# Two-block mixer: the first block's scores on stacked float32r operands, A heads between their projections, output weights read by halves

## The chip, the cores and the metric

The kernel runs on one core of a Trainium2 chip. The metric is device time in microseconds for one execution. PE is TensorE's matmul stream, PEld its weight loads, DVE VectorE, ACT ScalarE, POOL GpSimd and SP the engine that issues most loads. TensorE is granted one of two clock levels, 1.2 or 2.4 GHz; the profile shows the granted share, 0.50 or 1.00.

## The reference

512 tokens of width 1024 pass a first block and then a larger second block. Only the first block changes here. Its mixer has 8 "A" heads and 8 "B" heads of 64 features (B: two groups with one key/value head each). Cut to what matters:

```python
aq, ak, av, bq, kc, vc, ksl, vsl, kw, vw, gl = split_columns(rms_norm(h) @ w_in)
o_a  = mixer_dilated(aq, ak, av)               # three dilations, 8 heads
o_c  = softmax(bq @ compress(kc).T) @ compress(vc)     # 31 compressed tokens
o_s  = softmax(bq @ ksl.T + bias) @ vsl                # selected blocks
o_w  = softmax(bq @ kw.T + bias) @ vw                  # window of 512
o_b  = sum of the three, weighted by gates of gl
h    = h + concat(o_a, o_b) @ w_out
h    = h + (silu(n @ w_gate) * (n @ w_up)) @ w_down     # n = rms_norm(h)
```

With 512 tokens every A head and every B branch is a causal softmax over 512 keys with a bias by distance, so all three kinds run through the same routine.

## The kernel before, in words

The products of the projections keep float32 accuracy by splitting each operand in a high and a low float32r part and adding three products (`mm3`, L154 to L156). The attention scores before the change don't: they are plain float32 products, which the trace shows as two PE instructions each.

The first block (`first_block`) goes in this order. The rows are normed and turned. `proj_N` makes the A values. `bias_rows` writes the bias of every head, skewed for later reads, to DRAM: four stores on ACT's own queue. Eight `proj_T` make the A queries `aqT` and keys `akT` (128 features, that is two heads, by 512 tokens); queries leave PSUM by one ACT instruction (L283), keys by one copy on whichever engine is chosen (L286). The accumulators have two PSUM buffers, the split weights four.

`heads_a(p)` attends query tiles 2p and 2p+1 of the A heads, two heads (e = 0, 1) at a time. For a query tile i, `scores` (L373) makes the products with (i+1) x 128 keys (L377: 64 rows of the array, since a head has 64 features), adds the bias and takes the minimum on DVE (L382), the exponential on ACT (L383), turns the result on PE (L198) and copies it (L388). `values` multiplies with the values (L402), turns the reciprocal sums (L198) and splits the result for `w_out` on ACT and POOL (`split_late`). A pair is the four scores of two heads and two query tiles: widths 128, 128, 256, 256 at p = 0 and 384, 384, 512, 512 at p = 1. `attend` runs the turns a few scores late and slips the products with the values between the next scores.

After `heads_a(0)` come the windows of the compressed branch, the four B query projections `bqT`, `compress`, the gates, `heads_c` (scores against 32 compressed keys), and the keys `kslT` and `kwT`. Then one stream: `heads_a(1)`, `heads_b(0)` (8 pairs, two branches for each t), `heads_b(1)`. In `heads_b(0)`, `second_region` frees the A operands, loads the residual rows X (one 2 MB load on SP's queue) and makes `oc`, the compressed branch's output, in one go (`compressed`, L454, 32 rows of the array). `w_out(0)` and the feed-forward operand of the first 256 tokens stand at n = 3 of `heads_b(1)`, `w_out(1)` after it. Each `w_out(p)` reads all eight 512 KB chunks of the output weights, 16 chunk reads and splits in all, and adds both halves of the mix in one accumulation.

The written order is one of priority. The framework places the instructions of every engine ahead of time and lets later work fill an engine's gaps; products of `w_out(0)`, written in `heads_b(1)`, run between scores of `heads_a(1)`. Pools are buffers under a tag: an instruction that needs a buffer waits until an earlier user has released it. The feed-forward (from 433 us) also makes the modulation vectors of the second block, long vector work on DVE and POOL.

The second block's layers already use the stacked form: `stack_q`, `stack_k` and `qk` (L864) exist and serve their attention.

Of the kernel before, what the change touches and what calls it, by code (L numbers as in the profile page):

```python
# [77 lines left out]
class Act:  # L78
    """an operand with features on partitions, split in two exact parts; 512 lat tokens and 256 ctx tokens"""
# [15 lines left out]
class Kit:  # L95
    """Pieces shared by all phases: weight streaming, exact splits, products, norms."""
# [104 lines left out]
# =====================================================================  first block  # L201
def normed_T(K, ps_t, xs, nt, g, dst):
    """xs: normed rows of nt token tiles; transposed, times g per feature, split"""
# [11 lines left out]
def first_block(K, st, h_es):  # L215
    """x -> the first block's output in DRAM (K.dx), and the operand of layer 0's projections"""
# [34 lines left out]
    att = K.pool(att_es, "b1a")  # L251
    ap = K.pool(a_es, "b1ap", side="right")
# [20 lines left out]
    aqT = ap.tile([P, 4, S], F32, name="aqT")  # L273
    akT = ap.tile([P, 4, S], F32, name="akT")
    av = ap.tile([P, NT, 512], F32, name="av")
    bqT = proj.tile([P, 4, S], F32, name="bqT")
    kslT = proj.tile([P, S], F32, name="kslT")
    kwT = proj.tile([P, S], F32, name="kwT")
# [3 lines left out]
    def qevac(dst):  # L282
        return lambda ps: nc.scalar.activation(dst, ps, AF.Copy, scale=-0.125)  # L283

    def cevac(dst):
        return lambda ps: nc.any.tensor_copy(dst, ps)  # L286

    # ---- bias of every head by distance, for the skewed reads below
# [18 lines left out]
    # ---- compressed tokens: windows of 32 keys through a small MLP  # L307
# [6 lines left out]
    kcT = proj.tile([P, 32], F32, name="kcT")  # L314
# [5 lines left out]
    def windows(b):  # L320
        """overlapping windows of the raw keys or values, with their positions added"""
        cmpx = att.tile([P, 2, 512], F32, name="cmpx", tag="mhi", bufs=3)
# [9 lines left out]
        cmp[b] = att.tile([P, D], F32, name="blk", tag="mlo", bufs=3)[:, :992].rearrange("p (j g n) -> p j g n", j=16, g=2)  # L332
# [5 lines left out]
    def compress(b):  # L338
# [14 lines left out]
        if b == 0:  # L353
            for g in range(2):
                nc.tensor.matmul(ps2[64 * g:64 * g + 64, :32], cw2[:, 0], hid[:, g, 0], start=True, stop=True)
            nc.vector.tensor_copy(kcT, ps2[:, :32])
# [8 lines left out]
    def bias_tile(h, p):  # L365
        """(128, 256*(p+1)): negated bias of q tile 2p+1 against keys up to it"""
# [6 lines left out]
    def scores(qrow, krow, wb, i, fill, pt, den):  # L373
        """exponentials of q tile i of one head, transposed; fill puts work between"""
        w, ii = P * (i + 1), i % 2
        ps = ps_s.tile([P, 512], F32, name="sps", tag="s")
        nc.tensor.matmul(ps[:, :w], qrow[:, i * P:(i + 1) * P], krow[:, :w], start=True, stop=True)  # L377
# [12 lines left out]
    def pair(qT, ks, wbs, p, fill):  # L390
        """scores of two heads, q tiles 2p and 2p+1"""
        pts = [att.tile([P, 2 * p + 2, 256], F32, name="pt", tag="pt", bufs=4, padded_shape=[P, 4, 256]) for _ in range(2)]
        den = small.tile([P, 2, 2], F32, name="den", tag="den4", bufs=4)
        return [scores(qT[64 * e:64 * e + 64], ks[e], wbs[e], 2 * p + i, fill, pts[e], den[:, i, e:e + 1])
# [12 lines left out]
    def mix_tile(half, p):  # L407
        mix[half, p] = [att.tile([P, 4, 256], F32R, name=n, tag=n, bufs=3) for n in ("mhi", "mlo")]
        return mix[half, p]

    def heads_a(p, fill):
        m = mix_tile(0, p)

        def values(t, pts, den):
# [3 lines left out]
            split_late(K, m[0][:, t], m[1][:, t], weigh(K, att, po, rw))  # L418

        for t in range(4):  # L420
            sc, pts, den = pair(aqT[:, t], [akT[64 * e:64 * e + 64, t] for e in range(2)],
                                [bias_tile(2 * t + e, p) for e in range(2)], p, fill)
            yield sc, values(t, pts, den)

    def heads_b(p, fill):
# [3 lines left out]
        def values(t, br, pts, den):  # L429
# [9 lines left out]
            if br:  # L439
                nc.gpsimd.tensor_tensor(ys[0], ys[0], oc[:, t, 256 * p:256 * p + 256], op=OP.add)  # L440
                nc.gpsimd.tensor_tensor(ys[1], ys[1], ys[0], op=OP.add)
                split_late(K, m[0][:, t], m[1][:, t], ys[1])

        for t in range(4):
            wbs = [bias_tile(8 + 4 * g + t, p) for g in range(2)]
            for br, kT in ((0, kslT), (1, kwT)):
                sc, pts, den = pair(bqT[:, t], [kT[64 * g:64 * g + 64] for g in range(2)], wbs, p, fill)
                yield sc, values(t, br, pts, den)

    def compressed():  # L450
        for t in range(4):
            po = ps_o.tile([P, 512], F32, name="po", tag="po")
            for g in range(2):
                nc.tensor.matmul(po[64 * g:64 * g + 64], vc[32 * t:32 * t + 32, g], ptc[32 * t:32 * t + 32, g],  # L454
                                 start=True, stop=True)
            nc.any.tensor_copy(oc[:, t], po)
# [4 lines left out]
    def heads_c(i):  # L461
        """compressed branch, q tile i, all heads"""
        s3 = att.tile([P, 8, 32], F32, name="cs", tag="cs", bufs=2, padded_shape=[P, 16, 32])
        for g in range(2):
            ps = ps_s.tile([P, 512], F32, name="sps", tag="s")
            rows = slice(64 * g, 64 * g + 64)
            for t in range(4):
                nc.tensor.matmul(ps[:, t * 32:t * 32 + 32], bqT[rows, t, i * P:(i + 1) * P], kcT[rows],
                                 start=True, stop=True)
# [24 lines left out]

    proj_N(io["w_av"], 512, lambda t, ps: nc.any.tensor_copy(av[:, t], ps))
    bias_rows()
    for t in range(4):
        proj_T(t, qevac(aqT[:, t]))
        proj_T(4 + t, cevac(akT[:, t]))
    fill = Fill(FILLA)  # L500
    attend(heads_a(0, fill), fill, LAG1)
    windows(0)
    windows(1)
    for t in range(4):
        proj_T(8 + t, qevac(bqT[:, t]))
# [6 lines left out]
    proj_T(14, cevac(kslT))  # L512
    proj_T(15, cevac(kwT))
    X_es, oc_es = ExitStack(), ExitStack()

    def second_region():
        nonlocal X, oc
        a_es.close()
        X = K.pool(X_es, "res", side="right").tile([P, NT, D], F32, name="X")
        K.load(X, io["x"].rearrange("(t p) d -> p t d", p=P))  # L520
        oc = K.pool(oc_es, "b1oc", side="right").tile([P, 4, S], F32, name="oc")
        compressed()

    X = oc = None

    def w_out(p):
        for ch in range(2):
            chunks = [K.weights(io["w_out"][ch, kp]) for kp in range(4)]
            ps = [acc() for _ in range(2)]
            for half in range(2):  # L530
                for ii in range(2):
                    sl = slice(ii * P, (ii + 1) * P)
                    K.moving(ps[ii], chunks[2 * half:2 * half + 2], 512, lambda k: [z[:, k, sl] for z in mix[half, p]],
                             half == 0, half == 1)
            for ii in range(2):
                xc = X[:, 2 * p + ii, ch * 512:(ch + 1) * 512]
                nc.vector.tensor_add(xc, xc, ps[ii])
# [10 lines left out]
    def stream():  # L548
        yield from heads_a(1, fill)
        for n, x in enumerate(heads_b(0, fill)):  # L550
            if n == 2:
                second_region()
            yield x
        for n, x in enumerate(heads_b(1, fill)):
            if n == WO_AT:
                w_out(0)
# [4 lines left out]
    w_out(1)  # L561
    oc_es.close()
# [3 lines left out]
    # ---- feed-forward  # L566
# [5 lines left out]
    def ff_half(f):  # L572
        """the products of the first 256 tokens"""
# [75 lines left out]
    # ---- last products, the last norm, and the operand of the second block's first layer  # L649
# [80 lines left out]
def mod_scale(K, st, l):  # L730
    """gain * (1 + scale) per feature, both conditions: (128, 8, 2)"""
# [9 lines left out]
def modulated_T(K, work, ps_t, xs, gs, cols, r, h, col):  # L741
    """normed rows xs of n token tiles -> transposed, modulated, split into columns col.. of h"""
# [26 lines left out]
def rope_tables(K, pool, gain, name):  # L769
    """gain row broadcast, and gain*cos, gain*sin for the lat tokens"""  # L770
# [10 lines left out]
def head_norm(K, work, ps, nh, tabs, t, out, other):  # L781
    """ps (128, nh*64): per-head norm with gain, and rope where t is a lat tile"""
# [25 lines left out]
class Keys:  # L808
    """keys of all six token tiles: normed per head and turned at once, then stacked"""
# [1620 lines left out]
```

## Time and profile before

| | |
|---|---|
| runs, us | 2207.58, 2215.30, 2216.91; median 2215.3 |
| span of the profiled execution, us | 2212.8 |
| PE, PEld busy | 86%, 63% |
| DVE, ACT, POOL busy | 68%, 45%, 36% |
| first block's attention and output product | about 82 to 433 us |
| its feed-forward, with the modulation | from 433 us |

The profile records the span of its execution and no time around it; the median of the runs is 2.5 us above that span. A matmul's shown length overlaps that of its neighbour, so the cost of an instruction on PE is read from the start of one to the start of the next. A PE shown as fully busy is not at its peak: at half the granted clock the same products take longer and PE still counts as busy.

### The profile page before, as it was taken

How to read it: one execution, taken by the hardware profiler on the slowest of the kernel's cores; microseconds unless marked ns; L12 is line 12 of the kernel's file. 1: busy time of each engine (PE TensorE's matmuls, PEld its weight loads, DVE VectorE, ACT ScalarE, POOL GpSimd, SP SyncE). 2: the span in 40 equal slices, each digit the busy share in tenths (PEclk: the TensorE clock that was granted, in tenths of full speed). 3: DMA queues.
4: the chain of work that ended last, by engine and by line, in shares of the span. 5: the costliest groups of instructions: out<-in, count | busy, mean ns of one | idle time of the engine just before them, and what ended most of it. 6: DMA issues, size and time to landing. Idle time of an engine off the chain costs nothing. (4 is left out here: it accounts for less than half of the span.)

```text
span 2212.8 us, 27011 instructions
## 1 busy us (share of the span) xinstructions
PE 1907.1 (86%) x9478; PEld 1395.8 (63%) x9478; DVE 1509.1 (68%) x2516; ACT 1000.7 (45%) x1791; POOL 802.6 (36%) x486
## 2 busy tenths in 40 slices
PE   7699999987978878989988999588867899968887
PEld 5577446675756656767876677566645666755564
DVE  4145435598899887544448644799978877468878
ACT  3143434454443543443325732355634467335563
POOL 0000111274467544101122122376744511237664
PEclk9899759998988998979999999799987999979898
DMA  5432113355556565233210044488842100549773
GB/s 176 153 116 86 58 29 105 109 164 194 176 189 206 172 200 171 70 103 105 85 59 1 21 157 168 160 303 290 300 180 76 49 1 11 230 145 299 265 224 125
DMA packets 100204, 316.89 MB, mean 143 GB/s; under 512 B 15936, under 2 KB 19648, under 8 KB 100048
## 3 DMA queue, kind: packets, MB, share of 16 engines
q1 hardware_dynamic: 79296, 271.64, 37.1%
q0 software_dynamic: 8480, 20.98, 2.8%
q10 hardware_dynamic: 12272, 22.34, 2.7%
q8 instruction: 78, 1.28, 0.2%
q14 instruction: 78, 0.64, 0.1%
HBM read 293.28 MB, written 36.32 MB: 149 GB/s over the span
## 5 line engine op out<-in xcount | busy, mean ns | idle before, releaser
L149 DVE TENSOR_TENSOR wlo<-wraw,whi 128x1024 fp32r<-128x1024 f32 (+1 forms) x277 | 429.8, 1563 | 187.1 <-ACT whi L148 181.0
L148 ACT CAST whi<-wraw 128x1024 fp32r<-128x1024 f32 (+1 forms) x349 | 361.0, 1045 | 340.6 <-PE yo L156 88.2
L686 POOL TENSOR_TENSOR macc<-macc,xs 128x1024 f32<-128x1024 f32 x84 | 253.2, 3039 | 176.4 <-ACT xs L685 90.2
L156 PE MATMUL acc<-ahi,wlo 128*128 128x512 f32 (+1 forms) x576 | 218.7, 380 | 24.9 <-DVE wlo L149 24.9
L154 PE MATMUL acc<-ahi,whi 128*128 128x512 f32 (+1 forms) x576 | 218.8, 382 | 21.8 <-ACT aqT L283 19.8
L155 PE MATMUL acc<-alo,whi 128*128 128x512 f32 (+1 forms) x576 | 217.8, 378 | 0.0
L149 POOL TENSOR_TENSOR wlo<-wraw,whi 128x1024 fp32r<-128x1024 f32 x72 | 192.8, 2683 | 66.7 <-ACT whi L148 66.4
L687 DVE SCALAR_TENSOR_TENSOR macc<-wraw,silu,macc 128x1024 f32<-128x1024 f32 x84 | 200.9, 2415 | 8.2 <-DMA wraw<-mod_w 8.0
L909 POOL COPY rw<-rd 128x256 f32<-128x256 f32 x52 | 21.5, 414 | 367.2 <-DVE rd L915 263.9
L685 ACT ACTIVATE xs<-wraw,silu 128x1024 f32<-128x1024 f32 x84 | 94.7, 1148 | 121.4 <-DMA wraw<-mod_w 109.4
L156 PEld LDWEIGHTS acc<-ahi,wlo 128*128 128x128 f32 x576 | 111.4, 193 | 47.0 <-DVE wlo L149 28.1
L154 PEld LDWEIGHTS acc<-ahi,whi 128*128 128x128 f32 x576 | 111.0, 194 | 44.1 <-ACT aqT L283 20.2
L198 PE MATMUL tr<-ident,sc 128*128 128x128 f32 x752 | 137.6, 302 | 0.5 <-ACT pt L2100 0.5
L198 PEld LDWEIGHTS tr<-ident,sc 128*128 128x128 f32 x752 | 86.3, 148 | 72.2 <-issue 50.9
L155 PEld LDWEIGHTS acc<-alo,whi 128*128 128x128 f32 x576 | 111.6, 194 | 18.8
L156 PE MATMUL gu<-whi,xlo 128*128 128x512 f32 (+1 forms) x264 | 108.3, 410 | 7.0 <-DVE xlo L160 6.9
L154 PE MATMUL gu<-whi,xhi 128*128 128x512 f32 (+1 forms) x264 | 110.8, 420 | 0.8 <-ACT xhi L160 0.7
L154 PE MATMUL acc<-whi,ahi 128*128 128x512 f32 (+2 forms) x288 | 106.5, 374 | 5.3 <-DVEq L1198 5.3
L155 PE MATMUL gu<-wlo,xhi 128*128 128x512 f32 (+1 forms) x264 | 107.6, 407 | 1.0 <-DVE wlo L149 1.0
L156 PE MATMUL acc<-whi,alo 128*128 128x512 f32 (+2 forms) x288 | 104.9, 369 | 1.5 <-DVE alo L753 1.5
L155 PE MATMUL acc<-wlo,ahi 128*128 128x512 f32 (+2 forms) x288 | 104.9, 367 | 0.8 <-DVE wlo L149 0.8
L154 PE MATMUL dacc<-whi,fhi 128*128 128x512 f32 x176 | 79.7, 453 | 27.1 <-DVE X L624 20.1
(532 smaller groups left out, 4488.4 us busy)
## 6 DMA issues: line engine op xcount, KB each, us to landing
wraw<-ew SPq DMA_DIRECT2D x198, 512.0 KB
wraw<-mod_w SPq DMA_DIRECT2D x96, 512.0 KB
wraw<-w_gate SPq DMA_DIRECT2D x22, 512.0 KB
wraw<-w_up SPq DMA_DIRECT2D x22, 512.0 KB
wraw<-w_down SPq DMA_DIRECT2D x22, 512.0 KB
wraw<-yD SPq DMA_DIRECT2D x20, 512.0 KB
wraw<-w_s SPq DMA_DIRECT2D x16, 512.0 KB
wraw<-w_out SPq DMA_DIRECT2D x16, 512.0 KB
```

Of the source, the lines that this page charges most:

```text
L148: nc.scalar.copy(hi[:, :n], raw[:, :n])
L149: (eng or nc.vector).tensor_tensor(lo[:, :n], raw[:, :n], hi[:, :n].bitcast(F32), op=OP.subtract)
L154: mm(out, a[0], b[0], start=start, stop=False)
L155: mm(out, a[0], b[1], start=False, stop=False)
L156: mm(out, a[1], b[0], start=False, stop=stop)
L198: self.nc.tensor.transpose(out, src, self.ident[:n, :n])
L685: nc.scalar.activation(y, w, AF.Copy, scale=s0)
L686: nc.gpsimd.tensor_tensor(acc[:, 0, i], acc[:, 0, i], y, op=OP.add)
L687: nc.vector.scalar_tensor_tensor(acc[:, 1, i], w, s1, acc[:, 1, i], op0=OP.mult, op1=OP.add)
L909: K.nc.gpsimd.tensor_copy(rw, r[:, :, :, None].to_broadcast([P, 2, 2, 64]))
```

## The change

Scores become two float32r products. `stack_q` puts a head's scaled queries as a high part into 64 rows and the low part into the other 64, `stack_k` puts the high keys on both halves of the rows and the low keys on both halves of a second tile; `qk` multiplies the stacked queries with both and accumulates. This holds for the A heads, both B branches and the compressed scores (`kc`).

The A heads are no longer all projected first. `project(t)` makes the queries and keys of two heads; two are made ahead, and after both p of head pair t, `project(t + 2)` follows. `heads_a` runs p = 0 and p = 1 for each t, all before the windows. X has a pool from the start, and its load follows `heads_a`. B queries and keys live in a pool that takes the place of the A operands. The windows' two tiles move to the tag `pt` (four buffers, shared with the turned exponentials and the chunks of `compress`), and the mix tiles have two buffers where they had three.

`w_out(half, p)` reads only the four chunks of one half of the mix: the A half for all four query tiles ahead of `heads_b`, the B half at n = 3 of `heads_b(1)` for p = 0 and at the end for p = 1; 12 chunk reads, 16 additions to X where there were 8. The compressed output is made per t and p, in a buffer of the turns, and added on DVE from PSUM; `oc`, its copies and one POOL addition per t and p go.

```diff
-    def scores(qrow, krow, wb, i, fill, pt, den):
+    def scores(q, kk, e, wb, i, fill, pt, den):
...
-        nc.tensor.matmul(ps[:, :w], qrow[:, i * P:(i + 1) * P], krow[:, :w], start=True, stop=True)
+        qk(K, ps[:, :w], q[:, i * P:(i + 1) * P], kk[0][:, e], kk[1][:, e], slice(0, w))
...
+    def queries(i, Q):
+        proj_T(i, lambda ps: stack_q(K, ps.rearrange("p (n q) -> p n q", n=1), Q, slice(0, S)))
+    def keys(pool, i, name, bufs=1):
+        kk = [pool.tile([P, 2, S], F32R, name=name + z, tag=name + z, bufs=bufs) for z in "hl"]
+        proj_T(i, lambda ps: stack_k(K, ps, *kk, slice(0, S)))
+        return kk
...
-        mix[half, p] = [att.tile([P, 4, 256], F32R, name=n, tag=n, bufs=3) for n in ("mhi", "mlo")]
+        mix[half, p] = [att.tile([P, 4, 256], F32R, name=n, tag=n, bufs=2) for n in ("mhi", "mlo")]
...
+        def project(t):
+            Q = ap.tile([P, 2, 1, S], F32R, name="aq", tag="aq", bufs=2)
+            queries(t, Q)
+            return Q, keys(ap, 4 + t, "ak", 2)
...
+        ahead = [project(t) for t in range(2)]
         for t in range(4):
-            sc, pts, den = pair(aqT[:, t], [akT[64 * e:64 * e + 64, t] for e in range(2)],
-                                [bias_tile(2 * t + e, p) for e in range(2)], p, fill)
-            yield sc, values(t, pts, den)
+            Q, kk = ahead.pop(0)
+            for p in range(2):
+                sc, pts, den = pair(Q[:, :, 0], kk, [bias_tile(2 * t + e, p) for e in range(2)], p, fill)
+                yield sc, values(t, p, pts, den)
+            if t < 2:
+                ahead.append(project(t + 2))
...
             if br:
-                nc.gpsimd.tensor_tensor(ys[0], ys[0], oc[:, t, 256 * p:256 * p + 256], op=OP.add)
                 nc.gpsimd.tensor_tensor(ys[1], ys[1], ys[0], op=OP.add)
                 split_late(K, m[0][:, t], m[1][:, t], ys[1])
+            else:
+                oc = compressed(t, p)
+                nc.vector.tensor_add(ys[0], ys[0], oc)
...
+    def compressed(t, p):
+        ps = ps_t.tile([P, 512], F32, name="oc", tag="tr")[:, :256]
+        for g in range(2):
+            nc.tensor.matmul(ps[64 * g:64 * g + 64], vc[32 * t:32 * t + 32, g],
+                             ptc[32 * t:32 * t + 32, g, 256 * p:256 * p + 256], start=True, stop=True)
+        return ps
...
+    def w_out(half, p):
+        for ch in range(2):
+            chunks = [K.weights(io["w_out"][ch, 2 * half + kp]) for kp in range(2)]
+            for pp in p:
+                for ii in range(2):
+                    sl = slice(ii * P, (ii + 1) * P)
+                    ps = acc()
+                    K.moving(ps, chunks, 512, lambda k: [z[:, k, sl] for z in mix[half, pp]])
+                    xc = X[:, 2 * pp + ii, ch * 512:(ch + 1) * 512]
+                    nc.vector.tensor_add(xc, xc, ps)
...
-    for t in range(4):
-        proj_T(t, qevac(aqT[:, t]))
-        proj_T(4 + t, cevac(akT[:, t]))
     fill = Fill(FILLA)
-    attend(heads_a(0, fill), fill, LAG1)
+    attend(heads_a(fill), fill, LAG1)
+    K.load(X, io["x"].rearrange("(t p) d -> p t d", p=P))
+    a_es.close()
+    bp = K.pool(b_es, "b1b", side="right")
+    bq = bp.tile([P, 2, 4, S], F32R, name="bq")
...
-    proj_T(14, cevac(kslT))
-    proj_T(15, cevac(kwT))
+    ksl = keys(bp, 14, "ks")
+    kw = keys(bp, 15, "kw")
+    w_out(0, range(2))
...
-        yield from heads_a(1, fill)
-        for n, x in enumerate(heads_b(0, fill)):
-            if n == 2:
-                second_region()
-            yield x
+        yield from heads_b(0, fill)
         for n, x in enumerate(heads_b(1, fill)):
             if n == WO_AT:
-                w_out(0)
+                w_out(1, (0,))
                 ffn_operand(0, ffn_rows(0, att))
             yield x
     attend(stream(), fill, LAG1)
-    w_out(1)
+    w_out(1, (1,))
```

The rest of the diff renames operands to fit and removes comments.

## Rows read from the trace of the kernel before

**Rows 1.** The page's 40 slices: the granted TensorE clock in tenths of full speed.

```profile
PEclk9899759998988998979999999799987999979898
```

**Rows 2.** Busy us of PE, PEld, DVE, ACT, POOL per stretch, clock, DMA, GB/s.

```profile
122.60:127.11 4.51, 4.51 (x25) 2.47 (x25) 2.67 (x17) 3.18 (x12) 1.03 (x3) 1.00 0.39 91
...
252.45:297.32 44.87, 44.87 (x138) 22.03 (x136) 14.94 (x71) 17.50 (x62) 7.52 (x13) 0.50 0.09 25
257.86:265.75 7.89, 7.89 (x25) 3.96 (x24) 2.67 (x13) 3.40 (x12) 1.80 (x3) 0.50 0.07 18
297.32:340.47 43.15, 43.15 (x107) 18.25 (x107) 13.99 (x42) 13.00 (x36) 4.44 (x8) 0.50 0.07 19
309.49:322.93 13.44, 13.44 (x34) 5.44 (x33) 4.37 (x13) 5.30 (x14) 1.86 (x3) 0.50 0.08 21
383.59:391.84 8.25, 8.25 (x42) 3.65 (x41) 5.71 (x15) 3.61 (x11) 1.85 (x3) 1.00 0.00 0
...
432.99:900.00 467.01, 391.15 (x1699) 304.49 (x1700) 395.82 (x286) 201.14 (x222) 257.02 (x90) 0.90 0.57 181
```

**Rows 3.** The same view in the second block's layer-1 attention.

```profile
1784.00:1884.00 100.00, 100.00 (x717) 68.51 (x717) 77.81 (x215) 72.31 (x192) 14.00 (x25) 1.00 0.04 12
```

**Rows 4.** PE in order of time, full clock: start us, us, instruction, count.

```profile
121.82 0.48 PE L377 MATMUL sps<-akT,aqT 64*128 64x128 f32 x2
122.23 0.44 PE L198 MATMUL tr<-ident,sc 128*128 128x128 f32 x2
122.60 0.70 PE L377 MATMUL sps<-akT,aqT 64*128 64x256 f32 x2
123.23 0.65 PE L402 MATMUL po<-pt,av 128*64 128x256 f32 x4
...
223.47 1.12 PE L377 MATMUL sps<-akT,aqT 64*128 64x512 f32 x2
224.52 0.65 PE L402 MATMUL po<-pt,av 128*64 128x256 f32 x4
```

**Rows 5.** PE in order of time in the second block's layer-0 attention.

```profile
1246.41 0.36 PE L865 MATMUL sps<-Kh,Q 128*128 128x256 f32 x1
...
1246.81 0.65 PE L1283 MATMUL po<-pt,avN 128*64 128x256 f32 x4
...
1253.40 0.48 PE L865 MATMUL sps<-Kh,Q 128*128 128x512 f32 x1
...
1253.95 0.28 PE L865 MATMUL sps<-Kh,Q 128*128 128x256 f32 x1
```

**Rows 6.** PE in order of time: neighbouring scores of two heads; the compressed branch.

```profile
112.51 0.49 PE L377 MATMUL sps<-akT,aqT 64*128 64x128 f32 x4
112.93 0.50 PE L154 MATMUL acc<-ahi,whi 128*128 128x512 f32 x1
...
247.51 1.07 PE L454 MATMUL po<-ptc,vc 32*64 32x512 f32 x4
248.52 0.48 PE L377 MATMUL sps<-kslT,bqT 64*128 64x128 f32 x2
```

**Rows 7.** ACT, then PE, in order of time around the bias rows.

```profile
48.13 33.48 ACTq L133 DMA_DIRECT2D bf<-bd  x4
81.66 1.08 ACT L283 ACTIVATE aqT<-acc 128x512 f32<-128x512 f32 x2 [38.43 <-issue]
...
56.83 0.47 PE L154 MATMUL acc<-ahi,whi 128*128 128x512 f32 x1 [0.87 <-DVE akT L286]
...
62.15 0.39 PE L156 MATMUL acc<-ahi,wlo 128*128 128x512 f32 x1
82.31 0.79 PE L154 MATMUL acc<-ahi,whi 128*128 128x512 f32 x1 [19.77 <-ACT aqT L283]
```

**Rows 8.** Groups by line and shape, first 560 us: count, busy us, mean ns, idle before.

```profile
L328 DVE COPY cmpx<-acc 64x512 f32<-64x512 f32 x2 | 1.4, 683 | 3.8 <-PE acc L156 3.8
...
L286 DVE COPY akT<-acc 128x512 f32<-128x512 f32 x4 | 2.8, 692 | 20.4 <-PE acc L156 20.4
```

More of the change, by code (lines that the diff above doesn't have):

```diff
@@ L251, in first_block @@
     att = K.pool(att_es, "b1a")
+    X_es, b_es = ExitStack(), ExitStack()
+    X = K.pool(X_es, "res", side="right").tile([P, NT, D], F32, name="X")
     ap = K.pool(a_es, "b1ap", side="right")
@@ L271, in proj_N @@
             evac(t, ps[:, :width])
-    aqT = ap.tile([P, 4, S], F32, name="aqT")
-    akT = ap.tile([P, 4, S], F32, name="akT")
     av = ap.tile([P, NT, 512], F32, name="av")
-    bqT = proj.tile([P, 4, S], F32, name="bqT")
-    kslT = proj.tile([P, S], F32, name="kslT")
-    kwT = proj.tile([P, S], F32, name="kwT")
     bvn = proj.tile([P, NT, 256], F32, name="bvn")
     gate = proj.tile([P, NT, 24], F32, name="gate")
[L282 to L286, printed above, removed]
+    def queries(i, Q):
[4 more added lines that the diff above has]
+        return kk
     bd = K.dram.tile([16, 640], F32, name="bd")
@@ L313, in first_block @@
     K.store(cw2, io["cmp_w2"])
-    kcT = proj.tile([P, 32], F32, name="kcT")
+    kc = [proj.tile([P, 2, 32], F32R, name="kc" + z) for z in "hl"]
     vc = proj.tile([P, 2, 64], F32, name="vc")
@@ L320, in windows @@
     def windows(b):
-        cmpx = att.tile([P, 2, 512], F32, name="cmpx", tag="mhi", bufs=3)
+        cmpx = att.tile([P, 2, 512], F32, name="cmpx", tag="pt", bufs=4)
         nc.vector.memset(cmpx[64:128, :, 511:512], 0.0)
@@ L331, in windows @@
         proj_T(12 + b, shifted)
-        cmp[b] = att.tile([P, D], F32, name="blk", tag="mlo", bufs=3)[:, :992].rearrange("p (j g n) -> p j g n", j=16, g=2)
+        cmp[b] = att.tile([P, D], F32, name="blk", tag="pt", bufs=4)[:, :992].rearrange("p (j g n) -> p j g n", j=16, g=2)
         for g in range(2):
@@ L355, in compress @@
                 nc.tensor.matmul(ps2[64 * g:64 * g + 64, :32], cw2[:, 0], hid[:, g, 0], start=True, stop=True)
-            nc.vector.tensor_copy(kcT, ps2[:, :32])
+            stack_k(K, ps2[:, :32], *kc, slice(0, 32))
         else:
@@ L388, in scores, with pair @@
         nc.any.tensor_copy(pt[:, :i + 1, ii * P:(ii + 1) * P], ps[:, :w].rearrange("p (k q) -> p k q", q=P))
-    def pair(qT, ks, wbs, p, fill):
+    def pair(q, kk, wbs, p, fill):
         pts = [att.tile([P, 2 * p + 2, 256], F32, name="pt", tag="pt", bufs=4, padded_shape=[P, 4, 256]) for _ in range(2)]
         den = small.tile([P, 2, 2], F32, name="den", tag="den4", bufs=4)
-        return [scores(qT[64 * e:64 * e + 64], ks[e], wbs[e], 2 * p + i, fill, pts[e], den[:, i, e:e + 1])
+        return [scores(q[:, e], kk, e, wbs[e], 2 * p + i, fill, pts[e], den[:, i, e:e + 1])
                 for i in range(2) for e in range(2)], pts, den
@@ L407, in mix_tile, with heads_a, values @@
     def mix_tile(half, p):
-        mix[half, p] = [att.tile([P, 4, 256], F32R, name=n, tag=n, bufs=3) for n in ("mhi", "mlo")]
+        mix[half, p] = [att.tile([P, 4, 256], F32R, name=n, tag=n, bufs=2) for n in ("mhi", "mlo")]
         return mix[half, p]
-    def heads_a(p, fill):
-        m = mix_tile(0, p)
-        def values(t, pts, den):
+    def heads_a(fill):
+        ms = [mix_tile(0, p) for p in range(2)]
+        def project(t):
+            Q = ap.tile([P, 2, 1, S], F32R, name="aq", tag="aq", bufs=2)
+            queries(t, Q)
+            return Q, keys(ap, 4 + t, "ak", 2)
+        def values(t, p, pts, den):
             rw = inverse(K, att, den)
@@ L417, in values @@
             yield from products(po, [av[:, :, (2 * t + e) * 64:(2 * t + e + 1) * 64] for e in range(2)], pts, p)
-            split_late(K, m[0][:, t], m[1][:, t], weigh(K, att, po, rw))
+            split_late(K, ms[p][0][:, t], ms[p][1][:, t], weigh(K, att, po, rw))
+        ahead = [project(t) for t in range(2)]
         for t in range(4):
-            sc, pts, den = pair(aqT[:, t], [akT[64 * e:64 * e + 64, t] for e in range(2)],
-                                [bias_tile(2 * t + e, p) for e in range(2)], p, fill)
-            yield sc, values(t, pts, den)
+            Q, kk = ahead.pop(0)
[4 more added lines that the diff above has]
+                ahead.append(project(t + 2))
     def heads_b(p, fill):
@@ L439, in values @@
             if br:
-                nc.gpsimd.tensor_tensor(ys[0], ys[0], oc[:, t, 256 * p:256 * p + 256], op=OP.add)
                 nc.gpsimd.tensor_tensor(ys[1], ys[1], ys[0], op=OP.add)
                 split_late(K, m[0][:, t], m[1][:, t], ys[1])
+            else:
+                oc = compressed(t, p)
+                nc.vector.tensor_add(ys[0], ys[0], oc)
         for t in range(4):
             wbs = [bias_tile(8 + 4 * g + t, p) for g in range(2)]
-            for br, kT in ((0, kslT), (1, kwT)):
-                sc, pts, den = pair(bqT[:, t], [kT[64 * g:64 * g + 64] for g in range(2)], wbs, p, fill)
+            for br, kk in enumerate((ksl, kw)):
+                sc, pts, den = pair(bq[:, :, t], kk, wbs, p, fill)
                 yield sc, values(t, br, pts, den)
-    def compressed():
-        for t in range(4):
[L452 to L456, printed above, removed]
+    def compressed(t, p):
[4 more added lines that the diff above has]
+        return ps
     cmask = proj.tile([P, NT, 32], F32, name="cmask")
@@ L465, in heads_c @@
             ps = ps_s.tile([P, 512], F32, name="sps", tag="s")
-            rows = slice(64 * g, 64 * g + 64)
             for t in range(4):
-                nc.tensor.matmul(ps[:, t * 32:t * 32 + 32], bqT[rows, t, i * P:(i + 1) * P], kcT[rows],
-                                 start=True, stop=True)
+                qk(K, ps[:, t * 32:t * 32 + 32], bq[:, g, t, i * P:(i + 1) * P], kc[0][:, g], kc[1][:, g], slice(0, 32))
             nc.vector.tensor_tensor(s3[:, 4 * g:4 * g + 4], ps[:, :P].rearrange("p (h n) -> p h n", h=4),
@@ L493, in vevac @@
         nc.vector.reciprocal(e, e)
+    def w_out(half, p):
[8 more added lines that the diff above has]
+                    nc.vector.tensor_add(xc, xc, ps)
     proj_N(io["w_av"], 512, lambda t, ps: nc.any.tensor_copy(av[:, t], ps))
     bias_rows()
-    for t in range(4):
-        proj_T(t, qevac(aqT[:, t]))
-        proj_T(4 + t, cevac(akT[:, t]))
     fill = Fill(FILLA)
-    attend(heads_a(0, fill), fill, LAG1)
+    attend(heads_a(fill), fill, LAG1)
[3 more added lines that the diff above has]
+    bq = bp.tile([P, 2, 4, S], F32R, name="bq")
     windows(0)
@@ L504, in first_block @@
     for t in range(4):
-        proj_T(8 + t, qevac(bqT[:, t]))
+        queries(8 + t, bq[:, :, t:t + 1])
     compress(0)
@@ L511, in first_block @@
         heads_c(i)
-    proj_T(14, cevac(kslT))
-    proj_T(15, cevac(kwT))
[L514 to L537, printed above, removed]
+    ksl = keys(bp, 14, "ks")
+    kw = keys(bp, 15, "kw")
+    w_out(0, range(2))
     xn = K.act_lat()
@@ L560, in first_block @@
     attend(stream(), fill, LAG1)
-    w_out(1)
-    oc_es.close()
+    w_out(1, (1,))
+    b_es.close()
     att_es.close()
```

## Prediction

> **What bounds the kernel now.** I read the clock by slices first, then the busy time by stretches, then PE in order of time. The clock stands below 1.00 in most slices, but one stretch is longer and deeper than the rest: two neighbouring tenths of 0.7 and 0.5 in the fifth and sixth slice, some 55 us each [rows 1]. The stretches place it. From 252.45 to 340.47 us, 88.0 us, the granted clock is 0.50 and PE is busy for every microsecond, while DVE and ACT are busy for about a third of it [rows 2]. That is the stream of `heads_b(0)` and the first pairs of `heads_b(1)`. So PE bounds this stage, at the lower level, 1.2 GHz. Outside it, the pairs shown at full clock are PE-bound too (4.51 of 4.51 us, 8.25 of 8.25 us) [rows 2].
>
> What precedes the fall is in the order of PE: the compressed branch, products on 32 rows of the array, the first of them taking 1.01 us [rows 6]. The last pass of these ends at 252.45, where the window of clock 0.50 begins. The pairs of `heads_a` before it, made of the same float32 scores, ran at 1.00. At half clock a pair never brings the clock back; it rises in `w_out(0)`, near 340 us.
>
> The feed-forward is another regime: DVE busy 395.8 of 467.0 us [rows 2]. It starts when the first block's mixer is done and takes its work with it, so what the mixer gains should reach the end.
>
> **The change part by part.**
>
> Scores. At full clock a float32 score takes, from its start to that of the next product, 0.41 us at width 128, 0.63 at 256 and 1.05 at 512 [rows 4]; 384 lies between at 0.84. One of each is 2.93 us. The stacked form is in the trace, in the second block: width 256 takes 0.40 us for both products, width 512 0.55 before another stacked product [rows 5]. Behind a 512 here comes a different kind, so I take 0.60, a twentieth more than shown; 384 is then 0.50, and 128, which no row shows, 0.30 on the same line. One of each is 1.80. There are 32 A scores and 64 B scores, 24 of each width: 24 x (2.93 - 1.80) = 27.1 us. The bounds of the unknown 128: 0.30, and 0.62 if each of its two products were as slow per column as the float32 form (slope (1.05 - 0.41) / 384 = 1.67 ns, so 2 x 128 x 1.67 + 0.2). The upper end costs 24 x 0.32 = 7.7 us more. I take the line, since the nearest row, 256, is on it.
>
> What speaks against stacking is in the same order of PE: where two heads' scores stand side by side, four instructions of width 128 take 0.42 us, as much as two alone [rows 6]. Heads on rows 0 to 63 and 64 to 127 ran together. That happens for 4 of the 48 couples of scores (widths 128, 256, 384, 384), so the saving above counts 0.41 + 0.63 + 0.84 + 0.84 = 2.7 us that was never paid: 24.4 us remain.
> The Trainium skill's page "TensorE: Matmul & The Clock Gate", Part 3, section "The mechanism", says that products in different row groups run concurrently, and the row agrees. By it alone, all couples side by side would cost 24 x 2.93 / 2 = 35.2 us, less than the 43.2 of the stacked form; the order here lets only four do so.
>
> Clock. Pairs at p = 0 take 7.89 us at half and 4.51 at full clock, at p = 1 13.44 and 8.25 [rows 2]. The 44.87 us of p = 0 would be 44.87 x 4.51 / 7.89 = 25.6 at full clock, the 43.15 us of p = 1 (with some dense products) 43.15 x 8.25 / 13.44 = 26.5: 35.9 us less. I take all of it. The block of 32-row products is gone, spread in eight pieces; `heads_b` now follows dense projections and 96 products of `w_out(0)`; and layer 1's attention, built of the stacked scores, the same transposes and value products, holds 1.00 for 100 us with PE always busy [rows 3]. Lower bound: nothing, if the clock falls anyway (below).
>
> The start. The four bias stores occupy ACT's queue for 33.48 us, until 81.66 [rows 7]. Before, the first key leaves PSUM by DVE (PE resumes at 56.83 on its release), so a third projection runs in the shadow, 56.83 to 62.15; PE then waits 19.77 us for ACT to empty the queries [rows 7]. A stacked key needs ACT. Two projections fill both PSUM buffers, and the third moves behind the wait: 24 products at 5.32 / 23 us, 5.55 us. The buffer also comes free later: two half-height ACT instructions, of 0.54 each if like the two that take 1.08, then DVE's low part, 0.68 by the nearest copy [rows 7, 8], so at about 83.4 instead of 82.31. Together +6.7 us; 0 if the order hides one, 10 if the key's four ACT instructions come first.
>
> Other evacuations. A query costs two ACT and two DVE instructions where it cost one, a key four and four where it cost one; 64 rows take as long as 128 (683 and 692 ns) [rows 8]. A key is 2.2 us of ACT and 2.7 us of DVE, hidden under the next projection's 5.5 us on PE. Without that cover, 14 projections at some 2 us would be 28 us.
>
> Compressed output. Four times 1.01 us at most [rows 6] become eight pieces of half the columns, 0.5 to 1.0 each: 0 to +4 us, I take +1. Eight DVE additions replace eight on POOL and the copies, within DVE's slack: 2.67 of 4.51 us and 5.71 of 8.25 us per pair now [rows 2], against new PE pairs of 4.51 - 0.22 - 0.46 = 3.83 and 8.25 - 0.68 - 0.90 = 6.67. DVE then fills 86% of the longer pair and ACT 83% of the shorter; covered, with little room.
>
> Output weights. 192 products before and after. Four chunks fewer are read, split on ACT and DVE, both off the path; eight more additions hide under the 96 dense products. Nothing. The tail is shorter by half of `w_out(1)`, so that waiting for the last split may show: 0 to 2 us, taken as 0.
>
> Queues and buffers. X's load passes the windows' and B's weight loads and bias tiles on SP; they queue behind its issue and share its 2 MB, 11.6 us at the 181 GB/s of [rows 2], under A's last pairs and the chunks already fetched. If that cover failed, PE would wait about that long. Windows now wait for `pt` buffers of A's last pairs, and behind them their PSUM evacuation and B's projections: at most one pair, 6.67 us, filled by the scores still running. Two mix buffers make `heads_b`'s first split wait for all of `w_out(0)`, which stands ahead of it on PE. I take nothing for these three.
>
> Sum: -24.4 - 35.9 + 6.7 + 1 = -52.6 us. The profiled span, 2212.8, is 2.5 below the median of the runs; from that median, 2215.3 - 52.6 gives 2163 us.
>
> **The rivals.**
>
> A, the clock falls in `heads_b` after all. For: p = 0 has the smallest scores, and the stacked form makes them shorter still, leaving a larger share to transposes and weight loads; half clock did not end there before. Against: layer 1. Price, from the start of `heads_b(0)` to `w_out(1)` at n = 3: at the half-to-full ratios 1.75 and 1.63, eight pairs x 3.83 x 0.75 = 23, three x 6.67 x 0.63 = 13: 36 us back, 2199. Falling midway gives values between.
>
> B, ACT, DVE or the buffers take over, and the pairs keep their old full-clock times. For: the two shares of 83 and 86%. Against: layer 1, DVE 78 and ACT 72 of 100 us, without PE idling [rows 3]. The 24.4 us of scores are lost: 2187.
>
> C, slower: the lower level takes hold in the A heads already and lasts. All 24 pairs would run at half: 12 x 3.83 x 0.75 + 12 x 6.67 x 0.63 = 85 us, 2248. It decides once more than 53 us come back, that is when about five of every eight pairs run at half. Against: A's pairs lie between dense projections, and `heads_a` holds 1.00 now.
>
> D, no change: the feed-forward begins earlier but waits for its loads or DVE as long as before. For: DVE is its bound. Against: DVE's work there starts with the stage. 2215.
>
> **How the numbers follow.** Forecast 0.69, A 0.15, B 0.08, C 0.03, D 0.05. The forecast's own range takes the start's 0 to 10 us, the 128's 7.7, the compressed branch's 4 and the tail's 2: 2153 to 2178. B and most of A reach to 2195; above lie some of A, C and D, below almost nothing: 2153 to 2195. What this kernel's runs can tell from no change is about 0.5%, 11 us; all but C and D clear it: faster 0.92, same 0.05, slower 0.03.
>
> **What would show it.** Right: clock 1.00 where `heads_b` runs, PE always busy there, pairs near 3.8 and 6.7 us, PE idle from about 56 to 83 us, the feed-forward starting near 381 us. Wrong: clock 0.50 in `heads_b(0)` (A), PE waiting for DVE or ACT between scores (B), 128-wide stacked scores at 0.6 us, PE idle in front of the windows or `w_out(0)`.

## The result and the profile after

The changed kernel took 2157.06 us, median of 4 runs (2153.46 to 2161.67), beside 2213.66 us for the kernel before on the same chip: ratio 0.9752, 95% interval 0.9727 to 0.9778. The forecast was 2163 us. The profiled execution has a span of 2158.9 us, 53.9 less than before. A ratio leaves out executions more than 1.5% above the fastest of the same kernel, so where a kernel keeps the clock in some executions only (experiments 2 and 4), its single times say more than its ratio.

The clock by slices on the page of the changed kernel, against [rows 1]:

```profile
PEclk9799999999989879889999998799978999978898
```

The fifth and sixth slice went from 0.7 and 0.5 to 0.9 and 0.9: the long stretch at the lower level is gone. By stretches, from 83.55 us, where PE goes on with its projections after the bias stores, to the feed-forward:

```profile
core 0: us, PE busy (x) PEld busy (x) DVE busy (x) ACT busy (x) POOL busy (x), PEclk, DMA share, GB/s
83.50:130.00 46.50, 44.98 (x218) 34.09 (x219) 28.02 (x63) 27.57 (x66) 3.01 (x6) 0.94 0.45 144
...
232.00:258.00 26.00, 24.36 (x109) 19.34 (x108) 14.39 (x28) 7.39 (x13) 0.00 (x0) 1.00 0.25 79
258.00:288.00 30.00, 28.22 (x183) 17.68 (x181) 22.72 (x100) 21.97 (x81) 6.52 (x13) 1.00 0.25 71
288.00:324.00 36.00, 34.73 (x188) 22.71 (x187) 24.47 (x66) 22.49 (x55) 6.27 (x13) 1.00 0.24 64
324.00:338.00 14.00, 12.07 (x42) 5.97 (x43) 6.15 (x15) 5.21 (x13) 1.48 (x2) 0.63 0.33 102
338.00:367.00 29.00, 29.00 (x200) 17.19 (x198) 20.22 (x59) 16.39 (x42) 4.51 (x8) 1.00 0.12 38
367.00:380.00 13.00, 10.93 (x49) 7.82 (x45) 6.58 (x8) 5.85 (x8) 2.17 (x4) 1.00 0.33 102
sum 296.50, PE 285.39 PEld 207.85 DVE 180.01 ACT 159.44 POOL 29.90; mean PE 31.71 PEld 23.09 DVE 20.00 ACT 17.72 POOL 3.32
```

`heads_b` holds 1.00, except for 14 us where the operand of the feed-forward is turned; and PE is idle 11.1 of these 296.5 us (296.50 less 285.39). PE in order of time, a last column in brackets being the idle time before an instruction and its releaser:

```profile
82.02 0.48 PE L862 MATMUL sps<-akh,aq 128*128 128x128 f32 x1 [27.74 <-ACT akh L856]
83.55 0.76 PE L154 MATMUL acc<-ahi,whi 128*128 128x512 f32 x1 [1.06 <-DVE aq L845]
...
264.01 0.30 PE L862 MATMUL sps<-ksh,bq 128*128 128x128 f32 x1
...
264.60 0.65 PE L467 MATMUL oc<-ptc,vc 32*64 32x256 f32 x4
...
272.05 0.30 PE L862 MATMUL sps<-ksh,bq 128*128 128x128 f32 x1
...
284.58 0.30 PE L862 MATMUL sps<-kwh,bq 128*128 128x128 f32 x1
...
284.84 0.41 PE L198 MATMUL po<-ident,rw 128*128 128x128 f32 x2
...
343.50 0.42 PE L862 MATMUL sps<-kwh,bq 128*128 128x384 f32 x1
...
347.81 0.55 PE L198 MATMUL tr<-ident,sc 128*128 128x128 f32 x3
348.11 0.48 PE L862 MATMUL sps<-kwh,bq 128*128 128x512 f32 x1
...
349.64 0.42 PE L862 MATMUL sps<-ksh,bq 128*128 128x384 f32 x1
...
356.52 0.42 PE L862 MATMUL sps<-kwh,bq 128*128 128x384 f32 x1
...
380.08 0.36 PE L154 MATMUL acc<-ahi,whi 128*128 128x256 f32 x1 [1.69 <-ACT whi L148]
```

Two p = 0 pairs with one compressed piece take 8.04 us (264.01 to 272.05), a p = 1 pair 6.14, one with its piece 6.88. A stacked score of width 128 takes 0.26 us (284.58 to 284.84). The feed-forward starts at 380.08, before at 432.99: 52.9 us earlier. From there to the end both need the same, 1778.8 and 1779.8 us.

### The profile page after: what moved, and what is told of

It reads as the page before. It is cut to its first block, busy times and chain, and to the rows that moved or that the text cites. A ratio compares the mean times of both kernels' runs of the same rounds, so it can differ in the third digit from the quotient of the medians.

```text
span 2158.9 us, 27107 instructions
## 1 busy us (share of the span) xinstructions
PE 1835.9 (85%) x9494; PEld 1383.2 (64%) x9494; DVE 1527.1 (71%) x2559; ACT 1017.6 (47%) x1827; POOL 797.2 (37%) x478
## 3 DMA queue, kind: packets, MB, share of 16 engines
q8 instruction: 79, 1.29, 0.3%
## 5 line engine op out<-in xcount | busy, mean ns | idle before, releaser
L149 DVE TENSOR_TENSOR wlo<-wraw,whi 128x1024 fp32r<-128x1024 f32 (+1 forms) x273 | 423.8, 1565 | 139.6 <-ACT whi L148 135.8
L198 PE MATMUL tr<-ident,sc 128*128 128x128 f32 x752 | 129.7, 289 | 2.2 <-DVE alo L212 0.7
```

The source lines that it names most:

```text
L149: (eng or nc.vector).tensor_tensor(lo[:, :n], raw[:, :n], hi[:, :n].bitcast(F32), op=OP.subtract)
L198: self.nc.tensor.transpose(out, src, self.ident[:n, :n])
```

## The experiments

Each ratio is to the kernel before, in the same rounds. "Kept" means that the clock did not stay at the lower level in `heads_b`; where there is no trace of a run, its time decides.

**1. `spread`: the block of compressed products alone.**

```
-                nc.gpsimd.tensor_tensor(ys[0], ys[0], oc[:, t, 256 * p:256 * p + 256], op=OP.add)
...
+            else:
+                oc = compressed(t, p)
+                nc.vector.tensor_add(ys[0], ys[0], oc)
...
-        compressed()
```

> The kernel before with the compressed output in eight pieces, each beside its pair, in place of the block; everything else (float32 scores, old order) as before. If the block of 32-row products brings the clock down, heads_b now stays at 1.00 and 36 us are gained: about 2214 - 36 = 2178 us. If the float32 score stream at p = 0 does it by itself, the clock falls to 0.50 a little later and the time stays within 5 us of 2214.

2170.34 us (2167.48 to 2174.75), 0.9808 [0.9779, 0.9838]. By stretches, then PE:

```profile
233.90:274.75 40.85, 40.85 (x226) 21.45 (x225) 24.02 (x110) 24.07 (x89) 8.81 (x16) 1.00 0.34 109
274.75:372.00 97.25, 97.25 (x466) 52.10 (x467) 60.12 (x142) 47.86 (x111) 11.88 (x21) 1.00 0.22 65
```

```profile
80.05 0.79 PE L154 MATMUL acc<-ahi,whi 128*128 128x512 f32 x1 [16.63 <-ACT aqT L283]
...
245.49 0.48 PE L377 MATMUL sps<-kslT,bqT 64*128 64x128 f32 x2
...
255.24 0.48 PE L377 MATMUL sps<-kslT,bqT 64*128 64x128 f32 x2
...
342.66 0.91 PE L377 MATMUL sps<-kwT,bqT 64*128 64x384 f32 x2
...
348.32 0.55 PE L198 MATMUL tr<-ident,sc 128*128 128x128 f32 x3
348.80 1.12 PE L377 MATMUL sps<-kwT,bqT 64*128 64x512 f32 x2
...
350.91 0.91 PE L377 MATMUL sps<-kslT,bqT 64*128 64x384 f32 x2
...
359.74 0.59 PE L377 MATMUL sps<-kwT,bqT 64*128 64x384 f32 x1
...
393.20 0.36 PE L154 MATMUL acc<-ahi,whi 128*128 128x256 f32 x1 [0.19 <-DVE X L537]
```

The same float32 scores, in the old order, run at 1.00 for all 138 us. The load of X, which in the kernel before runs beside the block (DMA share 0.88 to 0.99 from 246 to 252 us) and so could have been the cause, stands at the same place here (1.02 from 246 to 248 us) without a fall. With this edit of a few lines alone, 44 of the 57 us are there. PE resumes at 80.05 instead of 82.31, so the edit itself is worth (393.20 - 80.05) - (432.99 - 82.31) = -37.5 us.

**2. Float32 scores in the changed order: `f32_all`, `f32_b`, `f32_b_block`.**

```
-        qk(K, ps[:, :w], q[:, i * P:(i + 1) * P], kk[0][:, e], kk[1][:, e], slice(0, w))
...
+            nc.tensor.matmul(ps[:, :w], q[rows, i * P:(i + 1) * P], kk[rows, :w], start=True, stop=True)
```

> The changed kernel with plain float32 scores of 64 rows in both kinds of heads and in the compressed branch; its order, its output weights by halves and its compressed output in eight pieces stay. If the clock was kept by the order or by the end of the block of 32-row products, heads_b stays at a granted clock of 1.00, only the shorter scores are lost (24.4 us in my sum) and the first key can again leave by DVE (6.7 us back): 2157 + 24 - 7 = about 2174 us. If the stacked scores themselves keep the clock, heads_b falls to 0.50 as before and 36 us more are lost: about 2210 us. Pairs at p = 1 near 8.2 us in the first case, 13.4 in the second.

> The changed kernel with plain float32 scores in heads_b and in the compressed branch alone; A heads stay stacked, so the start stays as in the changed kernel (PE waiting some 28 us behind the bias stores). 64 of the 96 scores lose their gain: 2/3 of 24.4 = 16 us. Clock kept by the order or the missing block: 2157 + 16 = about 2173 us at 1.00. Clock kept by the stacked scores: 0.50 in heads_b, 36 us more, about 2209 us.

> As f32_b, with the compressed output again in one block of 32-row products before the third pair of heads_b(0). If the block brings the clock down where float32 scores follow, the clock is 0.50 from there to about the output weights of the first tokens and the time is some 36 us above f32_b, about 2209 us; if it does not, the time is that of f32_b within 4 us.

`f32_all` took 2204.70, 2172.17, 2207.04 and 2201.31 us (0.9887 [0.9802, 0.9971]); `f32_b` 2216.61, 2180.64, 2192.57, 2221.94 (0.9886 [0.9838, 0.9934]); `f32_b_block` nine times between 2215.38 and 2226.30 (1.0041 [1.0024, 1.0058]). So with `f32_all` both expected values occur, 2174 and 2210, in one kernel; `f32_b` spreads as much, with 2192.57 between its two, which no trace explains. The clock of float32 pairs in this order is kept in some executions and lost in the others, five of eight by their times, and in all nine with the block. That does not test the block: in the one trace of `f32_b_block` the clock has fallen before the block's first product. The profiled execution of `f32_all` lost it:

```profile
258.00:260.00 2.00, 2.00 (x10) 1.63 (x9) 0.37 (x1) 0.87 (x1) 0.00 (x0) 1.00 0.00 0
260.00:262.00 2.00, 0.87 (x6) 0.32 (x5) 1.79 (x3) 1.22 (x2) 0.00 (x0) 1.00 0.00 0
262.00:264.00 2.00, 1.54 (x7) 0.81 (x7) 2.00 (x9) 1.23 (x6) 0.00 (x0) 0.79 0.72 209
264.00:266.00 2.00, 2.00 (x7) 1.45 (x8) 1.10 (x7) 1.96 (x9) 0.00 (x0) 0.50 0.68 207
```

It falls where PE, after the dense products of `w_out(0)`, waits 1.42 us for the first pair's scores to leave PSUM, and rises only near 331 us. The changed kernel has nearly the same wait, 1.29 us at 259.90, and does not fall. Undoing the stacking thus costs 2172 - 2157 = 15 us where the clock is kept (one execution, and less what the start gets back) and some 47 where it is not.

**3. `add_block`: the block given back to the stacked scores.**

```
+            if n == 2:
+                block()
             yield x
```

> The changed kernel with a block of compressed products added (the same eight products of 32 rows and 512 columns that the kernel before has, at the same place before the third pair of heads_b(0), their result copied and not used); the eight pieces stay. The block itself is some 4 us. If the end of the block is what keeps the clock in the changed kernel, the granted clock falls to 0.50 behind it, and up to 36 us more are lost: about 2197 us. If the stacked scores keep it, the clock stays at 1.00 or recovers within some pairs: 2161 to 2167 us.

2159.24 us (2154.24 to 2163.93), 0.9757 [0.9730, 0.9784].

```profile
264.00:266.00 2.00, 2.00 (x13) 0.87 (x12) 1.07 (x5) 1.42 (x6) 0.05 (x1) 1.00 0.75 226
266.00:268.00 2.00, 1.98 (x7) 0.41 (x6) 0.30 (x2) 0.92 (x4) 0.35 (x1) 0.71 0.15 48
268.00:270.00 2.00, 2.00 (x9) 0.48 (x8) 0.00 (x0) 0.15 (x1) 0.00 (x0) 0.50 0.00 0
...
274.00:276.00 2.00, 2.00 (x10) 1.02 (x9) 0.77 (x3) 0.78 (x5) 0.00 (x0) 0.50 0.00 0
276.00:278.00 2.00, 2.00 (x15) 1.55 (x15) 1.03 (x5) 1.30 (x6) 0.00 (x0) 0.73 0.00 0
278.00:280.00 2.00, 2.00 (x13) 1.25 (x15) 1.48 (x9) 1.35 (x6) 0.97 (x2) 1.00 0.00 0
```

Its time can't be told from the changed kernel's 2157.06. In its trace the clock falls near 266.8 us, within the block (264.65 to 272.72) and with PE busy for 1.98 of 2.00 us, where the changed kernel holds 1.00; it is back about 10 us later, some 4 us after the block's last product, among stacked pairs. The float32 pairs of `f32_b_block`, where the clock had fallen at the entry already, stood at 0.50 from 262 to 360 us. So in the old order ending the block is enough; in the changed order the stacked scores hold the clock, and in this trace win it back against the block. Stacked scores in the old order, with its block, were not run.

**4. What makes float32 fall in the changed order: `f32_wo_later`, `spread_dense`, `f32_wo_early`.** The first and last move `w_out(0, range(2))` in `f32_all`, to n == 1 of `heads_b(0)` and to before `compress(0)`; the second takes A's second pass in `spread` ahead of the keys:

```
+    attend(heads_a(1, fill), fill, LAG1)
     proj_T(14, cevac(kslT))
```

> f32_all with w_out(0) moved from before the first pair of heads_b(0) to behind its scores. In f32_all PE waits 1.42 us for the first pair's scores to leave PSUM and the clock is 0.50 from there on, in most of its runs. Here the same wait is followed by 96 dense products. If that wait is what brings the clock down, heads_b now starts without one behind dense work and holds 1.00 in every run: about 2172 us, the fastest of f32_all. If float32 pairs at p = 0 fall by themselves in this order, it stays near 2203 us.

> As spread (the kernel before with the compressed output in eight pieces, float32 scores), and the second pass of A heads moved ahead of the two projections of B's keys, so that heads_b(0) enters behind dense products with nothing pending, as in the changed order. spread held 1.00 throughout in every run. If that entry (PE waiting about 1.4 us for the first pair) is why the changed order with float32 scores mostly runs at 0.50 in heads_b, the clock falls here too in most runs: about 2205 us. If the cause lies elsewhere, it holds: about 2172 us.

> f32_all with w_out(0) moved from directly before heads_b(0) to before the compressed branch's products, so that heads_b(0) follows the projections of B's keys, as in spread_dense, which held 1.00 in every run. If the 96 dense products of w_out(0) directly ahead of the first p = 0 pairs are what makes float32 scores fall in the changed order, the clock holds in most runs here: about 2172 us. If it is something else in that order, it falls in most runs: about 2203 us.

`f32_wo_later` kept it in one of ten runs (2185.36, the others 2202.76 to 2229.18; 0.9994 [0.9964, 1.0023]); that one was traced, and its float32 pairs fell and came back some 7 us later:

```profile
268.00:270.00 2.00, 2.00 (x7) 1.09 (x7) 1.03 (x6) 1.28 (x6) 0.00 (x0) 0.69 0.52 172
270.00:272.00 2.00, 2.00 (x6) 0.79 (x4) 0.94 (x4) 0.90 (x4) 0.40 (x1) 0.50 0.00 0
...
274.00:276.00 2.00, 2.00 (x9) 1.03 (x7) 0.22 (x1) 0.67 (x3) 0.00 (x0) 0.60 0.00 0
276.00:278.00 2.00, 2.00 (x12) 1.21 (x10) 1.68 (x9) 1.04 (x4) 0.60 (x2) 1.00 0.01 4
```

`spread_dense` kept it in all four, 2170.18 us (2168.47 to 2176.07; 0.9812 [0.9781, 0.9842]), but the planner wove dense products between its first scores and PE never waited there, so it did not make the entry it was meant to. `f32_wo_early` lost it in all twelve (2200.98 to 2223.11; 0.9987 [0.9966, 1.0007]): the place of `heads_b(0)` behind `w_out(0)` is not the reason either. In four traces that fell (`f32_all`, `f32_b`, `f32_b_block`, `f32_wo_early`) PE had waited in the first microseconds of `heads_b(0)`; but the trace of `f32_wo_later` falls with PE busy throughout, just behind the first compressed piece (32 rows, 266.84 to 268.40 us). `spread` passes eight such pieces at 1.00, so a fall doesn't need the wait, and a piece is not enough for one. What decides it for float32 in this order stays open.

**5. The start: `stores_pool`, `stores_early`, `stores_split`, `split_pool_tiles`.**

```
-            K.store(bf[h:h + 4], bd[h:h + 4, None, :].to_broadcast([4, P, 640]))
+            nc.gpsimd.dma_start(bf[h:h + 4], bd[h:h + 4, None, :].to_broadcast([4, P, 640]))
```

That is `stores_pool`. `stores_early` also calls `bias_rows()` ahead of the projection of A's values. `stores_split` adds to `stores_pool`:

```
-    bf = K.dram.tile([16, P, 640], F32, name="bf")
+    bf = [K.dram.tile([4, P, 640], F32, name="bf%d" % g) for g in range(4)]
...
     attend(heads_a(fill), fill, LAG1)
+    for g in range(2, 4):
+        bias_store(g)
```

`split_pool_tiles` adds to that the load of A's tiles by `nc.gpsimd.dma_start`.

> The changed kernel with its four bias stores issued from POOL's queue in place of ACT's; nothing else moves. In the changed kernel PE waits 27.7 us at 82.02 because ACT is held 32.8 us by these stores. If that hold is the price of the start, ACT empties the first query and key at once and PE waits only where the first bias tile comes late. The stores themselves move the same bytes in some 33 us from about 47 to 80 us, and the first pair of A heads follows four projections (4 x 5.5 us after about 55), so it needs its bias at about 70: some 10 us of waiting stay and about 18 us are gained, 2157 - 18 = 2139 us. If the bias tiles wait for all four stores and the weight loads share their bandwidth, nothing is gained: 2157 us.

> As stores_pool, and the bias rows are made ahead of the projection of A's values, so that the stores run under its 96 dense products. If the hold of ACT and the lateness of the bias were all that the start cost, the 27.7 us go: about 2130 us. If the stores take bandwidth from the first weight loads, which PE waits for there, part is given back in front of the value projection: up to about 2145 us.

> The changed kernel with the bias copy in four DRAM tiles of four heads; the two for the A heads are stored from POOL's queue at the old place, the two for the B heads behind the A heads. In stores_pool the 27.7 us behind ACT were gone, but 14.1 us of PE waits for bias tiles came in their place, since a bias tile waited for all four stores (landing at about 79 us) and the later ones stood behind weight loads on SP. Half the bytes land in about half the 27 us, at about 62 to 65 us, before the first pair is due at about 76: if the lateness of the bias was all that was left, both waits go and some 14 us more are gained on stores_pool, about 2138 us. If weights or ACT are then late instead, it stays near 2150 us.

> stores_split with the bias tiles of the A heads loaded through POOL's queue in place of SP's. In stores_split PE still waits 6.4 us at 85.41 for the first bias tile, which SP issues only at 81.6 behind ten weight loads, and 5.0 us more in the A heads. If the place behind the weight loads is the whole of it, both go: 11 us less, about 2129 us. If POOL, which then waits for free bias buffers ahead of its own copies of the factors and its low parts, holds up the value products instead, it stays near 2140 us or rises.

`stores_pool` 2152.12 us, 0.9717 [0.9697, 0.9737]; `stores_early` 2159.79, 0.9744 [0.9721, 0.9768]; `stores_split` 2140.37, 0.9682 [0.9658, 0.9707]; `split_pool_tiles` 2143.67, 0.9688 [0.9664, 0.9712]. The issue of the same four stores, on ACT in the changed kernel and on POOL in `stores_pool`:

```profile
47.48 32.79 ACTq L133 DMA_DIRECT2D bf<-bd  x4
```

```profile
48.17 4.62 POOL L306 DMA_DIRECT2D bf<-bd  x4 [35.16 <-DMA bd<-bt]
```

The 27.74 us wait is gone, but PE now waits 12.6 us in the A heads for scores that DVE has not yet taken from PSUM, mostly because DVE waits for late bias tiles (8.1 us of its own). The 14.1 in the expectation holds another 1.5 us of `heads_b`, which the changed kernel has too. The clock is below 1.00 in stretches where it was not. `stores_split` against `stores_pool`, from 200 to 270 us:

```profile
200.00:270.00 70.00, 67.08 (x316) 52.08 (x314) 42.49 (x118) 26.85 (x66) 2.44 (x5) 0.83 0.26 79
```

```profile
200.00:270.00 70.00, 66.76 (x382) 52.07 (x380) 48.24 (x147) 33.15 (x88) 4.15 (x9) 1.00 0.27 83
```

The first row is `stores_pool`. Splitting the stores gained the 12 us, but not as expected: the same waits stayed at 11.4 us, since SP issues the first bias tile only at 81.63, behind ten weight loads, whatever has landed. What differs most is the clock, 0.83 and 1.00 in these 70 us; whether the split stores cause that, no run shows. Loading the tiles through POOL cut the first wait from 6.39 to 2.54 us and left 8.9 in the A heads, no gain. `stores_early` waits 4.5 us for its own constants and 12.6 in the A heads. `stores_split` beats both kernels.

## Why the prediction came out, step by step

My theory was that the clock and the shorter scores carry the gain, less a loss at the start; the rivals were A (the clock falls anyway), B (other engines take over), C (slower) and D (no change). Between the profiles the forecast's -52.6 us became 380.08 - 432.99 = -52.9, but from terms that were off in both directions: -37.5 (clock and pieces), -34.6 (scores), +6.8 (start) and +12.4 (covers) stand where it had -34.9, -24.4, +6.7 and nothing. That scores too small and covers too cheap cancel to 0.3 us is luck. Two slips in its sums change nothing: the terms named for its own range give 2155 to 2179, not 2153 to 2178, and the upper price of a 128 comes to 0.63, not 0.62.

- **Clock and compressed pieces**, -35.9 + 1: measured -37.5 in `spread`. The reason was half right. I named the missing block, the dense products ahead of `heads_b` and layer 1's stacked attention. In the old order the missing block is enough. In the changed order it is not: float32 scores without the block, behind the same dense products, lost the clock in most executions (`f32_all`), and it is the stacked scores that hold it. That a pair at half clock never brings the clock back was too strong: stacked pairs did after about 10 us (`add_block`), float32 pairs after some 7 us in one trace (`f32_wo_later`) and after some 68 in another (`f32_all`).
- **Scores**, -24.4: this term was under-sized. At equal clock two p = 0 pairs with their piece went from 9.75 to 8.04 us and p = 1 pairs from 8.25 to 6.14, with a piece from 8.83 to 6.88: 4 x 1.71 + 4 x 2.11 + 4 x 1.95 = 23.1 us for the B heads alone, where my terms give 16 x 1.13 = 18.1 (the four couples side by side were all of A heads). The prices of the scores are not what was wrong: in the p = 1 pair they save 3.79 - 2.32 = 1.47 us, where I had 1.58, and the width 128 came at 0.26 for my 0.30. What I left out stands in front of the scores. The turn just ahead of a float32 score takes 0.48 us (348.32 to 348.80 in `spread`), the same turn ahead of a stacked one 0.30 (347.81 to 348.11), and all four scores of the pair show the same 0.17 to 0.18 us. A price read from the start of a score to the next start misses that. If A's eight pairs, which lie among projections, save the same per pair, they add 11.5, which makes 34.6.
- **Start**, +6.7: PE resumes 1.24 us later (83.55 against 82.31) with one projection of 5.55 less done: +6.8. `f32_all`, whose first key leaves by DVE, waits 20.02 us for ACT and has the third projection in the shadow again.
- **Covers at nothing**: this step failed by about 12 us. From the resumption to the feed-forward, less the moved projection, the changed kernel needs 296.5 - 5.5 = 291.0 us and `spread` 313.2: -22.2, where the scores give -34.6. PE's busy time bears the larger figure out: 311.3 us in `spread` against 285.4 - 5.5 here is 31.4 less, though more of it here is at the lower level. PE idles 11.1 us there, `spread` 1.8; the largest part stands in the view of PE's waits (us in all, times, longest):

```profile
PE po L403 <- ACT pt L389: 1.8, 2, 0.9
PE tr L198 <- DVE alo L212: 1.7, 3, 0.8
PE sps L862 <- DVE mn L383: 1.5, 2, 1.3
PE acc L154 <- DVE ksl L858: 1.2, 1, 1.2
PE acc L154 <- DVE aq L845: 1.1, 1, 1.1
```

  This is rival B in small pieces: key, query and operand evacuations that I had hidden under the next projection, and the first pair of `heads_b`, which starts with nothing pending. The 14 us at 0.63 cost some 4 more (an estimate: three quarters of them at the lower level, which takes 1.63 times as long [rows 2]). This fall, too, comes in some executions only: in `add_block`'s trace the same operand, with the same waits, is turned at 1.00 throughout.
- **Queues, output weights**: no row of the waits names the load of X or a weight of `w_out(0)`; only the last split of `w_out(1)` shows, 0.38 us at 369.84.
- **Rivals.** A did not happen in the four runs. Such a fall is real, but A's reason for it, that shorter stacked scores leave more to turns and weight loads, is the wrong way round: in this order the longer float32 scores lost the clock and the stacked ones held it. C's price was never paid. D falls with the equal remainders, 1778.8 and 1779.8 us. The Trainium skill's page "TensorE: Matmul & The Clock Gate", Part 3, section "The mechanism", on row groups that run concurrently agrees with [rows 6] (four instructions in 0.42 us, as long as two alone), but no run here tried side-by-side heads throughout.

## What to carry to other kernels

Look for what stands just ahead of a fall of the clock: here four passes of products on 32 rows within 5 us, and spreading them was worth 37.5 of the 52.9 us between the profiles. Where the clock is kept in some executions only, another form of the same product can be worth more for the clock (here some 32 us) than for its own time (15 us), so price both, and time several executions. When pricing a product, read the start of the instruction ahead of it too. When edits take a little more of idle engines, sum the small new waits that they make on the bounding engine: covers named one by one still lost 9 us together.

## What was not expected of the hardware

- One program, float32 scores in the changed order, took 2172 or 2201 to 2207 us from execution to execution, with or without the clock.
- PE was busy for every microsecond from 262 to 360 us in `f32_b_block` and had 0.50; PE idle for 1.29 us in the changed kernel kept 1.00. The busy share alone does not tell the granted clock.
- The turn just ahead of a 64-row float32 score took 0.48 us, ahead of a stacked score 0.30.
- Issuing four stores of 1280 KB held ACT for 32.79 us and POOL for 4.62.
